# Where the weight pieces of a float32 decoder lie in SBUF: stationary hi and lo pieces moved to other places modulo 512 bytes

## The chip, the core and the metric

The kernel runs on one core of a Trainium2 chip. The metric is the device time of one execution in microseconds (us). Before the change it is 609.66 us, the median of three runs (609.53 to 610.31).

## What is computed

Two decoder layers over 256 tokens of width 1024, in float32, and a last RMSNorm. Each layer normalises its input and projects it by one wide matrix (1024 x 9808). Three attention mixers of 8 heads work on the result, their outputs are multiplied by SiLU gates, projected by a matrix per branch, weighted by sigmoid gates, summed, projected once more and added to the input. Cut to what matters here:

```python
def hybrid_layer(x, gain, w_in, f_bias, w_branch, w_out):
    h = rms_norm(x, gain)
    proj = jnp.einsum('bsd,de->bse', h, w_in)                 # 1024 x 9808
    (qa, ka, va, ga, qb, kb_, vb_, gb, qc, kc, vc, gc,
     q_idx, k_idx, w_idx, f_logit, merge_logit) = jnp.split(proj, SPLIT_POINTS, axis=-1)
    ...
    y = jnp.einsum('nbsw,nwd->bsnd', jnp.stack([oa, ob, oc], axis=0), w_branch)
    gates = jax.nn.sigmoid(merge_logit).reshape(B, S, N_BRANCH, D_MODEL)
    merged = jnp.sum(gates * y, axis=2)
    return x + jnp.einsum('bsd,de->bse', merged, w_out)
```

## The kernel before

**Hi and lo pieces.** Every float32 weight is split into two float32r pieces: ACT copies the raw weights to a hi piece (L415), DVE subtracts hi from raw and writes the rest as a lo piece (L419). Activations are split likewise (hTh and hTl for the normalised input, og0h, og0l, og1h, og1l for the branch outputs). A product then takes three matmuls: hi with hi, hi with lo, lo with hi.

**Buffers.** The hi pieces go through a ring of six tiles wh0 to wh5, the lo pieces through wl0 to wl5, each of 1152 float32r numbers per partition (4608 bytes), of which a piece takes 1024. The raw weights arrive by DMA from SyncE in four tiles of 2048 numbers. In the program as built, the wh tiles begin at byte 128 modulo 512 of a partition and the wl tiles at 0. The tiles hTh, hTl and og0h to og1l begin at 192 modulo 512, the tiles v0 and v1 at 128. Below, "at 128" always means the byte address modulo 512 at which an operand begins. One block of 128 columns is 512 bytes, so all blocks of a piece begin at the same place.

**Two ways to use a piece.** Where the tokens are the output's rows (units of unit_a, first_v and va_units: the v projections and the output projection), the activation is stationary and the weight piece streams past it as the moving operand. Their places in the tile are set by the table MOVING, read by shifted (L393). Where the tokens are the output's columns, the weight piece is stationary, in blocks of 128 x 128, and 256 columns of an activation stream. These are the B units (unit_b at L469: queries, keys, gates, index queries and merge gates, 64 units a layer, 24 matmuls each, pieces from win_b) and the Y units (unit_y at L956: branch projections, 24 a layer, 12 matmuls each, pieces from wbr). Their pieces have no entry in the table: piece (L398) puts them at the beginning of the tile, so the stationary hi blocks begin at 128 and the lo blocks at 0, and what streams begins at 192.

In both layers together 3,072 matmuls are of B units and 576 of Y units, 3,648 in all, 1,824 in each layer. Two thirds of them have a hi block as their stationary operand. Before each, TensorE loads that block (LDWEIGHTS), beside the streaming of the matmul before.

**What sets the order.** A planner in the kernel places every operation by its own costs, due times and a table of shifts. In a B unit the 16 hi matmuls and 8 lo matmuls are mixed by UNIT_ORDER:

```python
UNIT_ORDER = ((6, 1), (3, 1), (3, 2), (2, 1), (1, 2), (1, 1))
```

that is six matmuls with hi, one with lo, three with hi, one with lo, and so on. Between units, TensorE computes the scores (tiles s, L678 and L680), the transposes of the probabilities (tile t, L766) and the products with v (tile o, L782 to L785).

Of the kernel before, what the change touches and what calls it, by code (L numbers as in the profile page):

```python
# [32 lines left out]

R_RING = 6
R_RAW = 4
MOVING = {"V": (192, 192), "C": (128, 0), "CK": (384, 384), "O": (128, 128)}
TAIL = {"ACT": 95.0, "DVE": 85.0, "POOL": 0.0, "PE": 0.0, "SP": 0.0}
STEP = 24.0
SPLIT_LEAD = 2.0
# [237 lines left out]
def hybrid_trunk(ctx, tc, x, w_in, w_branch, w_out, final_gain, consts, out):  # L277
    nc = tc.nc
    PE, ACT, DVE, POOL = nc.tensor, nc.scalar, nc.vector, nc.gpsimd
# [13 lines left out]
    def T(b):  # L293
        return b.slot[1]
# [28 lines left out]
    V = [pool.tile([128, 2, 8, 128], F32R, name=f"v{i}") for i in range(2)]  # L323
# [67 lines left out]

    chunks, pieces = {}, {}

    def shifted(kind):
        at = MOVING[kind]
        return [slice((a - base) % 512 // 4, (a - base) % 512 // 4 + 1024) for a, base in zip(at, (128, 0))]

    def piece(key, ckey, ap, cshape, sel, shape, k, at=(slice(0, 1024), slice(0, 1024))):  # L398
        if key in pieces:
            return pieces[key]  # L400
        if ckey not in chunks:
            c = chunks[ckey] = Buf("raw")
            ca, cb = cshape

            def load():
                c.v = T(c)[:, :ca * cb].rearrange("p (a b) -> p a b", a=ca)
                nc.sync.dma_start(c.v, ap)
            dma(load, 512 * ca * cb * (1 if cb >= 128 else 2), [], [c], k - 12, f"dma {ckey}")
        c = chunks[ckey]
        a, b = shape  # L410
        p = pieces[key] = (Buf("wh"), Buf("wl"))

        def hi():
            p[0].v = T(p[0])[:, at[0]][:, :a * b].rearrange("p (a b) -> p a b", a=a)
            ACT.activation(p[0].v, sel(c.v), AF.Copy)  # L415

        def lo():
            p[1].v = T(p[1])[:, at[1]][:, :a * b].rearrange("p (a b) -> p a b", a=a)
            DVE.tensor_tensor(p[1].v, sel(c.v), p[0].v.bitcast(F32), op=ALU.subtract)  # L419
        act(hi, a * b, False, [c], [p[0]], k - SPLIT_LEAD, f"hi {key}")  # L420
        dve(lo, a * b, [c, p[0]], [p[1]], k - SPLIT_LEAD, f"lo {key}", port=True)
        return p
# [6 lines left out]
    def rows_a(kind, w, l, c0, i, k):  # L429
        src = w[l][(i // 2) * 512:(i // 2 + 1) * 512, c0:c0 + 512].rearrange("(k p) c -> p k c", p=128)  # L430
        a = (i % 2) * 2
        return piece((kind, l, c0, i), (kind, l, c0, i // 2), src, [4, 512], lambda r: r[:, a:a + 2, :], [2, 512], k,
                     shifted("O" if kind == "O" else "V"))

    def wbr(l, n, j, k):
        src = w_branch[l][n][:, (j // 2) * 256:(j // 2 + 1) * 256].rearrange("(k p) c -> p k c", p=128)
# [26 lines left out]
    def unit(name):  # L463
        units[0] += 1
        return units[0] - 1
# [560 lines left out]
    hA = (lambda k, t: hTh[:, k, t * 128:(t + 1) * 128], lambda k, t: hTl[:, k, t * 128:(t + 1) * 128])  # L1026
# [16 lines left out]

    def first_v():

        us, at = [unit("va0"), unit("va1")], shifted("V")
        ps = [Buf("proj"), Buf("proj")]
        left, done = [24, 24], [[], []]
        raws = [Buf("raw"), Buf("raw")]
        for i in range(KC):  # L1050
            c = raws[i // 4]
            if i % 2 == 0:
                ph, pl = Buf("wh"), Buf("wl")
            v = lambda b, w, i=i: T(b)[:, at[w]][:, (i % 2) * 512:(i % 2 + 1) * 512]
            rv = lambda c=c, i=i: T(c)[:, (i % 4) * 512:(i % 4 + 1) * 512]
            src = w_in[0][i * 128:(i + 1) * 128, COL["va"]:COL["va"] + 512]
            kr, kh, kl = Tok(), Tok(), Tok()
            plan.op([("SP", 512 * 512 / 330.0, lambda rv=rv, src=src: nc.sync.dma_start(rv(), src))], [], [kr], -95 + 0.2 * i, LAND,
                    f"dma va{i}", touch=[c])
            key = W_KEY[0] + W_KEY[1] * i  # L1060
            if i:
                key = max(key, HT_KEY[0] + HT_KEY[1] * (i - 0.5))
            plan.op([("ACT", t_act(512, False), lambda v=v, rv=rv, ph=ph: ACT.activation(v(ph, 0), rv(), AF.Copy)),
                     ("DVE", t_dve2(512), lambda v=v, rv=rv, ph=ph: DVE.tensor_copy(v(ph, 0), rv()))],
                    [kr], [kh], key, 0.0, f"hi va{i}", touch=[c, ph])
            dve(lambda v=v, rv=rv, ph=ph, pl=pl: DVE.tensor_tensor(v(pl, 1), rv(), v(ph, 0).bitcast(F32), op=ALU.subtract),
                512, [kr, kh], [kl], key + 0.05, f"lo va{i}", touch=[c, ph, pl], port=True)
            for t in range(2):
                for w, h, kw, kx, n in ((ph, hA[0], kh, 0, 0), (ph, hA[1], kh, 1, 0), (pl, hA[0], kl, 0, 1)):
                    def emit(t=t, w=w, h=h, i=i, v=v, n=n):  # L1070
                        left[t] -= 1
                        PE.matmul(T(ps[t]), h(i, t), v(w, n), start=left[t] == 23, stop=left[t] == 0)  # L1072
                    k = Tok()
                    done[t].append(k)
                    pe(emit, t_mm(512), [kw, k_hT[kx][t][i]], [k], us[t] - 10, f"va{t}", touch=[ps[t], w])
        for t in range(2):
            v_out(ps[t], t, 0, done[t], us[t])

    def va_units(l, vi):

        fine = False
        us, ats = [unit(f"vc{h}{t}") for h in "lr" for t in range(2)], [shifted("C"), shifted("CK")]

        def rows(raw, c, n, k0, k1, key):
            tok = Tok()
# [4 lines left out]
            return tok  # L1090

        def split(p, n, w, c, x0, x1, raw, cols, k0, reads, toks, key):
            dst = lambda i: T(p[i])[:, ats[w > 256][i]][:, :n * w].rearrange("p (k c) -> p k c", k=n)[:, x0:x1, c:c + cols]
            src = lambda: T(raw)[:, :8 * cols].rearrange("p (k c) -> p k c", k=8)[:, k0 + x0:k0 + x1]
            m = (x1 - x0) * cols
            ways = [("ACT", t_act(m, False), lambda: ACT.activation(dst(0), src(), AF.Copy))]
            if fine:
                ways.append(("DVE", t_dve2(m), lambda: DVE.tensor_copy(dst(0), src())))
            plan.op(ways, reads + [k_hT[1][0][KC - 1]], toks[0], key, 0.0, "hi va", touch=[raw, p[0]])
            dve(lambda: DVE.tensor_tensor(dst(1), src(), dst(0).bitcast(F32), op=ALU.subtract), m, reads + toks[0], toks[1],  # L1100
                key + 0.5, "lo va", touch=[raw, *p], port=True)

        for side, (w, slots) in enumerate(((256, ((0, 4), (4, 8))), (336, ((0, 3), (3, 6), (6, 8))))):
            u = us[2 * side:2 * side + 2]
            ps = [Buf("proj"), Buf("proj")]
            left, done = [24, 24], [[], []]
# [9 lines left out]
            for i, (a, b) in enumerate(slots):  # L1116
                p, n = [Buf("wh"), Buf("wl")], b - a
                tk = [[Tok() for _ in range(n)] for _ in range(2)]
                hk = VA_HI[2 * side + i] if fine else u[0] - SPLIT_LEAD
                for x0, x1 in ((0, 2), (2, 4)) if fine and not side and not i else ((0, n),):  # L1120
                    split(p, n, w, 0, x0, x1, raw, 256, a, list({id(kr[a + x]): kr[a + x] for x in range(x0, x1)}.values()),
                          [tk[0][x0:x1], tk[1][x0:x1]], hk)
                kt2 = [[Tok()], [Tok()]]
                if side:
                    split(p, n, w, 256, 0, n, rk, 80, a, [kk], kt2, hk)
                for t in range(2):
                    for wi, hi in ((0, 0), (0, 1), (1, 0)):
                        for js in [(x,) for x in range(n)] if fine and not side and not i else (range(n),):
                            def emit(t=t, wi=wi, hi=hi, js=js, p=p, n=n, a=a, w=w, ps=ps, left=left):
                                for x in js:  # L1130
                                    left[t] -= 1
                                    PE.matmul(T(ps[t])[:, :w], hA[hi](a + x, t), T(p[wi])[:, ats[w > 256][wi]][:, :n * w].rearrange(  # L1132
                                        "p (k c) -> p k c", k=n)[:, x], start=left[t] == 23, stop=left[t] == 0)
                            k = Tok()
                            done[t].append(k)
                            pe(emit, len(js) * (t_mm(w) + 4.6), [tk[wi][x] for x in js] + (kt2[wi] if side else []) +
                               [k_hT[hi][t][a + x] for x in js], [k], u[t] - (10 if fine else 0), f"v{side}{t}", touch=[ps[t], p[wi]])
# [44 lines left out]
    for l in range(L):  # L1182
# [31 lines left out]
        for hh in range(2):  # L1214
            gets = [lambda k, i=i: rows_a("O", w_out, l, hh * 512, i, k) for i in range(4)]
            for t in range(2):
                ra = [lambda k, p=p: [k_mg[k][p]] for p in range(2)]
                cols = [(0, 256), (256, 256)] if last and hh + t == 2 else [(0, 512)]
                for i, (c, n) in enumerate(cols):
                    u, ps = unit_a(f"o{hh}{t}", gets, t, mA[0], mA[1], ra, c, n)  # L1220
# [38 lines left out]
```

## Time and profile before

| | |
|---|---|
| median of 3 runs | 609.66 us (609.53 to 610.31) |
| time of the profiled execution | 609.88 us |
| its span, first to last instruction | 607.9 us |
| granted TensorE clock | 0.998 |
| matmuls, weight loads in the trace | 4848 each |
| HBM read | 103.42 MB |

The profiled execution is 0.22 us above the median. Its time is the span and 2.0 us around it. PE stands for TensorE's matmuls, PEld for its weight loads, which run beside them. Matmuls are pipelined: one that streams 256 columns is recorded as 276 ns long, but the next one starts 113 ns after it, so what a matmul costs is read from the distance between starts. Starts are given to a hundredth of a microsecond, and so a distance is read over several matmuls.

### The profile page before, as it was taken

The numbers are of one execution on the slowest core, as the hardware profiler recorded it, in microseconds if no ns is written. First come the engines' busy times: TensorE is split into PE (matmuls) and PEld (weight loads), VectorE is DVE, ScalarE is ACT, GpSimd is POOL, SyncE is SP. The second block draws the span as 40 slices with busy tenths as digits, with TensorE's granted clock in tenths as the row PEclk, the third lists the DMA queues.
The fourth block names the chain that finished last, engine by engine and source line by source line (L and its number), as shares of the span: only waits on it lengthen the run. The fifth ranks groups of instructions, "written<-read, shape, count | busy, mean of one in ns | idle before, by whom it ended". The sixth has DMA issues, their size and how long they took to land.

```text
span 607.9 us, 12752 instructions
## 1 busy us (share of the span) xinstructions
PE 599.9 (99%) x4848; PEld 581.7 (96%) x4848; DVE 534.3 (88%) x1340; ACT 439.9 (72%) x933; POOL 89.7 (15%) x97
## 2 busy tenths in 40 slices
PE   8999999999999999999999999999999999999996
PEld 6999999999998999999889999999999999999985
DVE  8899999997998899979586999999889978999873
ACT  6668669697986678775585875987788756986641
POOL 1032052000000334100000520320000014220000
PEclk9999999999999999999999999999999999999999
DMA  9995384845454655284547547557448256445411
GB/s 305 296 312 183 90 240 140 252 134 188 140 174 139 208 173 173 88 274 163 160 141 255 159 139 234 166 183 228 128 118 278 92 175 204 144 139 183 165 35 70
DMA packets 98109, 107.39 MB, mean 177 GB/s; under 512 B 4352, under 2 KB 88960, under 8 KB 98048
## 3 DMA queue, kind: packets, MB, share of 16 engines
q1 hardware_dynamic: 97760, 106.15, 55.4%
q8 instruction: 38, 0.62, 0.4%
q10 hardware_dynamic: 288, 0.43, 0.2%
q14 instruction: 23, 0.19, 0.1%
HBM read 103.42 MB, written 1.05 MB: 172 GB/s over the span
## 4 chain that ended last, share of the span: by engine, by line
PE 97%; issue 1%; DMA 1%; DVE 0%; ACT 0%; POOL 0%; POOLq 0%; DVEq 0%; SPq 0%
PE proj L457 80%; PE proj L1132 4%; PE t L766 3%; PE s L680 2%; PE s L678 2%; PE proj L1072 2%; PE o L785 1%; PE o L782 1%; DMA xg<-in_x_dram 1%; PE o L784 0%; PE o L783 0%; PE t L580 0%; PE s L580 0%; POOL fsum L626 0%; ACT tmp L565 0%
## 5 line engine op out<-in xcount | busy, mean ns | idle before, releaser
L457 PE MATMUL proj<-hTh,wh 128*128 128x256 f32 x1024 | 266.6, 278 | 0.0
L457 PE MATMUL proj<-hTl,wh 128*128 128x256 f32 x1024 | 265.8, 277 | 0.0
L419 DVE TENSOR_TENSOR wl<-raw,wh 128x1024 fp32r<-128x1024 f32 x180 | 221.9, 1240 | 29.1 <-ACT wh L415 26.5
L457 PE MATMUL proj<-hTh,wl 128*128 128x256 f32 x1024 | 230.6, 278 | 0.0
L415 ACT ACTIVATE wh<-raw 128x1024 fp32r<-128x1024 f32 x180 | 190.0, 1058 | 54.9 <-PE proj L457 50.2
L457 PEld LDWEIGHTS proj<-hTh,wh 128*128 128x128 f32 x1024 | 192.4, 188 | 0.1
L457 PEld LDWEIGHTS proj<-hTl,wh 128*128 128x128 f32 x1024 | 192.3, 188 | 0.1
L457 PEld LDWEIGHTS proj<-hTh,wl 128*128 128x128 f32 x1024 | 173.5, 188 | 0.0
L507 POOL TENSOR_TENSOR rsh<-rsh,cst 128x256 f32<-128x256 f32 x40 | 32.9, 823 | 323.4 <-DVE rsh L506 271.5
L509 POOL TENSOR_TENSOR rr<-rr,rsh 128x256 f32<-128x256 f32 x40 | 48.0, 1199 | 5.1 <-DVE rr L508 2.0
L743 ACT ACTIVATE e<-e,st 128x128 f32<-128x128 f32 (+1 forms) x96 | 42.7, 447 | 6.6 <-DVE st L739 6.3
L457 PE MATMUL proj<-wh,v 128*128 128x512 f32 (+1 forms) x144 | 35.2, 366 | 0.0
L457 PE MATMUL proj<-og0l,wh 128*128 128x256 f32 x128 | 33.8, 276 | 0.0
L457 PE MATMUL proj<-og0h,wh 128*128 128x256 f32 x128 | 32.3, 276 | 0.0
L457 PEld LDWEIGHTS proj<-wh,v 128*128 128x128 f32 x144 | 25.3, 189 | 4.2
L457 PE MATMUL proj<-og0h,wl 128*128 128x256 f32 x128 | 28.6, 276 | 0.0
L771 DVE TENSOR_TENSOR ptl<-t,pth 128x384 fp32r<-128x384 f32 x48 | 24.8, 550 | 0.7 <-ACT pth L769 0.5
L457 PEld LDWEIGHTS proj<-og0h,wh 128*128 128x128 f32 x128 | 24.0, 188 | 0.0
L457 PEld LDWEIGHTS proj<-og0l,wh 128*128 128x128 f32 x128 | 24.0, 188 | 0.0
L800 DVE TENSOR_TENSOR ot<-o,ot 64x256 f32<-64x256 f32 x48 | 19.9, 415 | 3.8 <-ACT ot L798 3.4
L769 ACT ACTIVATE pth<-t 128x384 fp32r<-128x384 f32 x48 | 21.8, 482 | 0.4
L457 PEld LDWEIGHTS proj<-og0h,wl 128*128 128x128 f32 x128 | 21.7, 188 | 0.0
(225 smaller groups left out, 1098.5 us busy)
## 6 DMA issues: line engine op xcount, KB each, us to landing
raw<-in_w_in_dram SPq DMA_DIRECT2D x74, 1024.0 KB, 5.3
raw<-in_w_branch_dram SPq DMA_DIRECT2D x24, 512.0 KB, 3.6
raw<-in_w_out_dram SPq DMA_DIRECT2D x8, 1024.0 KB, 5.1
raw<-in_w_in_dram SPq DMA_DIRECT2D x8, 256.0 KB, 5.4
tmp<-wf SPq DMA_DIRECT2D x16, 128.0 KB, 6.5
raw<-in_w_in_dram SPq DMA_DIRECT2D x2, 320.0 KB, 7.6
x<-in_x_dram SPq DMA_DIRECT2D x2, 256.0 KB, 4.9
acc<-in_final_gain_dram SPq DMA_DIRECT2D x1, 512.0 KB, 3.6
```

Source lines behind the costliest of these rows:

```text
L415: ACT.activation(p[0].v, sel(c.v), AF.Copy)
L419: DVE.tensor_tensor(p[1].v, sel(c.v), p[0].v.bitcast(F32), op=ALU.subtract)
L457: PE.matmul(o(), a(), b(), start=first and i == 0, stop=last and i == n - 1)
L507: gps(lambda: POOL.tensor_tensor(T(sh)[:np_], T(sh)[:np_], s[:np_], op=ALU.mult), S, [k_rope], [sh], key, "rope")
L509: gps(lambda: POOL.tensor_tensor(T(r)[:np_], T(r)[:np_], T(sh)[:np_], op=ALU.add), S, [sh], [r], key, "rope")
L678: PE.matmul(o.rearrange("p (h c) -> p h c", h=2), qh[:, sl], kl[:, :, :n], start=True, stop=False)
L743: act(lambda t=t, a=a, n=n, e=e, st=st: ACT.activation(T(e)[:, a:a + n], T(e)[:, a:a + n], AF.Exp, bias=T(st)[:, t:t + 1], scale=-1.0, acc ...
L766: PE.transpose(T(ps)[:, i * 128:(i + 1) * 128], T(es[h])[:, i * 128:(i + 1) * 128], ident)
L769: act(lambda h=h, src=src: ACT.activation(T(ph)[:, h], src(), AF.Copy), 384, True, [ps], [kp[h][0]], key, "pT", touch=[ph])
L771: dve(lambda h=h, src=src: DVE.tensor_tensor(T(pl)[:, h], src(), T(ph)[:, h].bitcast(F32), op=ALU.subtract), 384, [ps, kp[h][0]], [kp[h][1 ...
L800: dve(lambda r=r, h=h: DVE.tensor_tensor(T(t)[r], T(o)[:64, h * S:(h + 1) * S], T(t)[r], op=ALU.add), S, [o], [kt[h]], key, "og", touch=[t ...
L1132: PE.matmul(T(ps[t])[:, :w], hA[hi](a + x, t), T(p[wi])[:, ats[w > 256][wi]][:, :n * w].rearrange("p (k c) -> p k c", k=n)[:, x], start=le ...
```

## The change

The table MOVING becomes PLACE, with an entry for each layer, and gets two more kinds: "B" and "Y", the stationary pieces. Their hi pieces now begin at 0 modulo 512 in both layers, their lo pieces at 128 in the first layer and at 64 in the second. The entries of the moving pieces (V, C, CK, O0, O1) repeat the old numbers in both layers. The function place gives the part of the tile from the wanted place to its end, and piece looks the place up by the kind of its key.

```diff
-MOVING = {"V": (192, 192), "C": (128, 0), "CK": (384, 384), "O": (128, 128)}
+PLACE = {"V": ((192, 192), (192, 192)),
+         "C": ((128, 0), (128, 0)),
+         "CK": ((384, 384), (384, 384)),
+         "O0": ((128, 128), (128, 128)),
+         "O1": ((128, 128), (128, 128)),
+         "B": ((0, 128), (0, 64)),
+         "Y": ((0, 128), (0, 64))}
...
-    def shifted(kind):
-        at = MOVING[kind]
-        return [slice((a - base) % 512 // 4, (a - base) % 512 // 4 + 1024) for a, base in zip(at, (128, 0))]
-
-    def piece(key, ckey, ap, cshape, sel, shape, k, at=(slice(0, 1024), slice(0, 1024))):
+    def place(kind, l):
+        at = PLACE[kind][l]
+        return [slice((a - base) % 512 // 4, 1152) for a, base in zip(at, (128, 0))]
+
+    def piece(key, ckey, ap, cshape, sel, shape, k):
+        at = place(key[0] if key[0] in PLACE else "V", key[1])
...
-        return piece((kind, l, c0, i), (kind, l, c0, i // 2), src, [4, 512], lambda r: r[:, a:a + 2, :], [2, 512], k,
-                     shifted("O" if kind == "O" else "V"))
+        return piece((f"{kind}{c0 // 512}" if kind == "O" else kind, l, c0, i), (kind, l, c0, i // 2), src, [4, 512], lambda r: r[:, a:a + 2, :], [2, 512], k)
```

The rest of the diff carries the layer to place in first_v and va_units. As built, the two programs are the same instruction for instruction on every engine, waits included: only addresses inside the wh and wl tiles differ. Stationary operands, before and after:

| stationary block | place before | place after, layer 1 | place after, layer 2 | matmuls per layer |
|---|---|---|---|---|
| hi, B and Y units | 128 | 0 | 0 | 1,216 |
| lo, B and Y units | 0 | 128 | 64 | 608 |

What streams past them begins at 192 before and after.

More of the change, by code (lines that the diff above doesn't have):

```diff
@@ L1044, in first_v @@
     def first_v():
-        us, at = [unit("va0"), unit("va1")], shifted("V")
+        us, at = [unit("va0"), unit("va1")], place("V", 0)
         ps = [Buf("proj"), Buf("proj")]
@@ L1081, in va_units, with rows_of @@
         fine = False
-        us, ats = [unit(f"vc{h}{t}") for h in "lr" for t in range(2)], [shifted("C"), shifted("CK")]
+        us = [unit(f"vc{h}{t}") for h in "lr" for t in range(2)]
+        def rows_of(p, i, n, w):
+            at = place("C" if w == 256 else "CK", l)[i]
+            return T(p[i])[:, at][:, :n * w].rearrange("p (k c) -> p k c", k=n)
         def rows(raw, c, n, k0, k1, key):
@@ L1092, in split @@
         def split(p, n, w, c, x0, x1, raw, cols, k0, reads, toks, key):
-            dst = lambda i: T(p[i])[:, ats[w > 256][i]][:, :n * w].rearrange("p (k c) -> p k c", k=n)[:, x0:x1, c:c + cols]
+            dst = lambda i: rows_of(p, i, n, w)[:, x0:x1, c:c + cols]
             src = lambda: T(raw)[:, :8 * cols].rearrange("p (k c) -> p k c", k=8)[:, k0 + x0:k0 + x1]
@@ L1131, in emit @@
                                     left[t] -= 1
-                                    PE.matmul(T(ps[t])[:, :w], hA[hi](a + x, t), T(p[wi])[:, ats[w > 256][wi]][:, :n * w].rearrange(
-                                        "p (k c) -> p k c", k=n)[:, x], start=left[t] == 23, stop=left[t] == 0)
+                                    PE.matmul(T(ps[t])[:, :w], hA[hi](a + x, t), rows_of(p, wi, n, w)[:, x], start=left[t] == 23, stop=left[t] == 0)
                             k = Tok()
```

## The prediction

> **What bounds the kernel now.** I read the page first, for the engine that sets the end.
>
> ```profile
> span 607.9 us, 12752 instructions
> PE 599.9 (99%) x4848; PEld 581.7 (96%) x4848; DVE 534.3 (88%) x1340; ACT 439.9 (72%) x933; POOL 89.7 (15%) x97
> PE 97%; issue 1%; DMA 1%; DVE 0%; ACT 0%; POOL 0%; POOLq 0%; DVEq 0%; SPq 0%
> ```
>
> PE is 97% of the chain that ended last, so time is gained or lost only where a matmul starts earlier or later. Next, the groups of PE by line, since the change touches one kind of matmul alone: those with wh or wl behind the comma, as the stationary operand.
>
> ```profile
> L457 PE MATMUL proj<-hTh,wh 128*128 128x256 f32 x1024 | 266.6, 278 | 0.0
> L457 PE MATMUL proj<-hTl,wh 128*128 128x256 f32 x1024 | 265.8, 277 | 0.0
> L457 PE MATMUL proj<-hTh,wl 128*128 128x256 f32 x1024 | 230.6, 278 | 0.0
> L457 PE MATMUL proj<-og0l,wh 128*128 128x256 f32 x128 | 33.8, 276 | 0.0
> ```
>
> These are the 3,072 matmuls of the B units and, with og, some of the 576 of the Y units. The last number before the bar's end is the mean duration of one. It is 276 to 278 ns for the same shape, so something makes some of them longer. The third view, all instructions on a tile in one stretch (minimum, median, maximum), tells when. First a stretch without scores or transposes:
>
> ```profile
> L457 PE MATMUL proj<-hTh,wh x51: 276/276/276, 200.0 to 219.9; 128*128 128x256 f32 x51
> L457 PE MATMUL proj<-hTl,wh x50: 276/276/276, 200.1 to 219.7; 128*128 128x256 f32 x50
> ```
>
> Then the microsecond behind a group of scores:
>
> ```profile
> L457 PE MATMUL proj<-hTh,wh x5: 278/279/280, 56.9 to 57.9; 128*128 128x256 f32 x5
> L457 PE MATMUL proj<-hTl,wh x4: 277/279/279, 57.0 to 57.8; 128*128 128x256 f32 x4
> ```
>
> The same instructions with the same places take 276 ns in the one and 279 in the other. The timeline of both shows what that does to the starts. The quiet stretch (first column: start):
>
> ```profile
> 200.00 0.28 PE L457 MATMUL proj<-hTh,wh 128*128 128x256 f32 x1
> ...
> 202.04 0.28 PE L457 MATMUL proj<-hTh,wl 128*128 128x256 f32 x1
> ```
>
> Here 18 matmuls start in 2.04 us: 113.3 ns each. And behind the scores:
>
> ```profile
> 56.86 0.28 PE L457 MATMUL proj<-hTh,wh 128*128 128x256 f32 x1
> 56.98 0.28 PE L457 MATMUL proj<-hTl,wh 128*128 128x256 f32 x1
> ...
> 57.45 0.28 PE L457 MATMUL proj<-hTl,wh 128*128 128x256 f32 x1
> 57.57 0.28 PE L457 MATMUL proj<-hTh,wl 128*128 128x256 f32 x1
> ...
> 57.92 0.28 PE L457 MATMUL proj<-hTh,wh 128*128 128x256 f32 x1
> 58.04 0.28 PE L457 MATMUL proj<-hTh,wl 128*128 128x256 f32 x1
> 58.15 0.28 PE L457 MATMUL proj<-hTl,wh 128*128 128x256 f32 x1
> 58.26 0.28 PE L457 MATMUL proj<-hTh,wh 128*128 128x256 f32 x1
> 58.38 0.28 PE L457 MATMUL proj<-hTl,wh 128*128 128x256 f32 x1
> ```
>
> From 56.86 to 58.04 ten matmuls start in 1.18 us: 118 ns each, 4.7 more than in the quiet stretch. From 58.04 on they start 113.3 ns apart again (three in 0.34 us). So there are two ways of running, a quiet one at 113.3 ns and bursts at 118. A burst begins where TensorE comes back from scores, transposes or products with v, and this one ends at the second matmul whose stationary operand is a lo block (58.04), not at the first (57.57). A lo block is the only thing in a burst that lies at another place, 0 instead of 128.
>
> Do places matter at all? Two stretches in which weights stream and the activation is stationary, also 256 columns, never become quiet:
>
> ```profile
> 21.24 0.63 PE L1132 MATMUL proj<-wh,hTh 128*128 128x256 f32 x4
> ...
> 24.07 0.63 PE L1132 MATMUL proj<-wh,hTh 128*128 128x256 f32 x4
> ```
>
> ```profile
> 596.31 0.64 PE L457 MATMUL proj<-wh,v 128*128 128x256 f32 x4
> ...
> 598.46 0.64 PE L457 MATMUL proj<-wh,v 128*128 128x256 f32 x4
> ```
>
> In the first, 24 matmuls take 2.83 us, 117.9 ns each, with the moving operand at 128 or 0 and the stationary one at 192. In the second, 18 take 2.15 us, 119.4 each, with both at 128. With the moving operand at 192 and the stationary one at 128 or 0, as in B and Y units, it stays quiet for 20 us. Distances from the stationary to the moving place of 64 and 192 bytes allow 113.3 ns; of 0, 448 and 320 (modulo 512) they were only seen at 118 to 120.
>
> **The change, part by part.** It adds and removes no instruction. Three parts have a price.
>
> *The quiet stretches.* After the change the distance is 192 for hi blocks and 64 for lo blocks in layer 1. Both were seen quiet, so I take 113.3 ns, nothing gained or lost. In layer 2 the lo blocks have a distance of 128, which no row shows with 256 columns. Its neighbours on both sides, 64 and 192, are quiet, so I take 0. The other end is 4.7 ns on each of the 608 lo loads of layer 2, 2.9 us, or on all its 1,824 matmuls, 8.6 us. A gain is excluded: no row shows a shorter distance than 113.3.
>
> *The bursts.* All that can be won is what the bursts cost now. The hTl row gives it, since its mean of 277 lies 1 ns above the quiet 276. Its rows over most of the span have no exceptionally long matmul, while those of hTh do:
>
> ```profile
> L457 PE MATMUL proj<-hTh,wh x1008: 276/276/365, 39.9 to 568.5; 128*128 128x256 f32 x168
> L457 PE MATMUL proj<-hTl,wh x1008: 276/276/285, 40.1 to 568.9; 128*128 128x256 f32 x168
> ```
>
> So 3,072 x 1 ns = 3.1 us, and as the mean is rounded, 1.5 to 4.6. Adding up the distances between starts of these 3,648 matmuls beyond 113.3 ns, record by record without the 42 long ones (362 to 365 ns, behind transposes, which no place explains), gives 2.2 us of excess. I use 2.2, as it is in the unit that counts. In a burst a hi block loaded behind a hi block keeps the 4.7 ns every time; the change of place that comes with a lo block is what ends it. After the change these steps exist in the same positions, with the opposite sign in layer 1 (0 to 128 and back instead of 128 to 0 and back) and half as large in layer 2. Bounds: if a load at 0 does not keep the distance of 118 ns, hardly a burst outlives its second matmul, and nearly all 2.2 us go; if the steps no longer end it, a burst lasts until its unit group ends, which is the end of 8.6 us a layer. Between them I take a quarter off the bursts, 0.55 us: two loads in three now lie where the burst above ended, which speaks for shorter bursts, and against it, that burst outlived its first load at 0.
>
> *The splits.* ACT and DVE write the pieces at the new places.
>
> ```profile
> L419 DVE TENSOR_TENSOR wl<-raw,wh 128x1024 fp32r<-128x1024 f32 x180 | 221.9, 1240 | 29.1 <-ACT wh L415 26.5
> L415 ACT ACTIVATE wh<-raw 128x1024 fp32r<-128x1024 f32 x180 | 190.0, 1058 | 54.9 <-PE proj L457 50.2
> ```
>
> ACT idles 50.2 us ahead of the hi pieces because PE has not yet given a tile back: the ring of six is full, and that is the cover. DVE's 29.1 us are a wait for ACT. Even 50 ns more on each of 180 pieces would be 9 us, less than that cover. I take 0. If the cover were gone, those 9 us would come into PE's path.
>
> The sum against the profiled execution: 609.88 - 0.55 = 609.3; against the median of the runs, which is 0.22 lower, 609.1 us.
>
> **A rule that speaks against any effect.** The rows above show 113.3 ns against 118 and 119.4 for the same number of columns. The Trainium skill, SBUF — State Buffer, "Who interferes with whom", lists two independent read ports for PE, one for the moving operand and one for LDWEIGHTS, and says that PE never waits on anyone. By that rule the places are free and the sum is 609.7 instead of 609.1; the trace agrees in the quiet stretch and does not explain the bursts. As a mechanism of this kernel it is the first rival.
>
> **The rivals.**
>
> *Places do nothing.* The bursts would then be the tail of every switch of operation: the pipeline needs some matmuls to get its lead back, whatever lies where. For it: a burst begins at a switch, and at the same places TensorE runs at 118 and then at 113.3. Against it: two stretches with other places never become quiet. Time 609.7. Chance 0.15.
>
> *The bursts go.* A load at 0 ends a burst at once, now that every hi block lies there. For it: the burst above ends with a load at 0. Against it: its first load at 0 did not end it. It gives 1.3 to 2.2 us, 607.5 to 608.4, most likely 607.9. Chance 0.32.
>
> *The 118 ns settle, in layer 2 above all.* The step between hi and lo is only 64 bytes there, and a burst that a step of 128 bytes needed two tries to end may then run through; or the untested distance of 128 is one of those that never become quiet. For it: the two stretches that stay at 118 or 119 have steps of 128 and of 0 between their pieces, so a step alone is no way out. Against it: both neighbours of the distance are quiet. Price 4.7 ns a matmul: 2.9 us if a third of layer 2 runs so, 612.5 us; 8.6 if all of it is. It decides from 260 matmuls on (1.2 us / 4.7 ns), 7% of the 3,648. Chance 0.20.
>
> That the change doesn't reach the hardware is excluded: the built program has the stationary blocks at the new places.
>
> **How the numbers follow.** A measurement of this kernel can tell about 0.2%, 1.2 us, from no change. My forecast, that bursts change by less than half and the rest stays, has 0.33, and lies inside 0.2% as does the first rival: same 0.48. The likeliest time is the forecast's, 609.1 us, its own range 608.4 to 610.4. Faster by over 0.2% is the second rival alone, 0.32; slower the third, 0.20. The range reaches down to 607.6, near the end of the second rival, since no more than the bursts can be won, and leaves some 0.05 below. Above it reaches 611.5, which takes in bursts that are almost doubled (1.8 us) and leaves the larger part of the third rival out, some 0.13.
>
> **What would show it.** Right: in the changed kernel's profile the stretch from 200 to 220 us has 276/276/276 again, the mean of the hTl row lies between 276 and 277, and PE's span is a few tenths of a microsecond shorter. For the second rival: the ten matmuls behind the scores near 56.9 us start 113 ns apart from the second one on. For the third: layer 2 (from some 310 us) has medians of 279 on wh or wl where layer 1 has 276. The splits would be wrong if PE waited for ACT or DVE at L457. The prediction is wrong if the median leaves 607.6 to 611.5, and its reasoning is wrong if the time falls by more than 2.2 us, since nothing here shows more to win.

## The result, and the profile after

The changed kernel takes 616.61 us (median of four runs, 616.4 to 616.73), the kernel before beside it 609.75: a ratio of 1.011 (95% interval 1.009 to 1.013). It is 6.9 us slower. The forecast was 609.1 us in a range of 607.6 to 611.5, so it was wrong, in its sign too.

The page of the changed kernel, the same rows as before:

```profile
span 614.5 us, 12752 instructions
PE 607.5 (99%) x4848; PEld 589.2 (96%) x4848; DVE 535.8 (87%) x1340; ACT 440.0 (72%) x933; POOL 89.4 (15%) x97
PE 97%; issue 1%; DMA 1%; DVE 0%; POOL 0%; ACT 0%; POOLq 0%; DVEq 0%; SPq 0%
```

PE is busy 7.6 us longer with the same 4848 matmuls and is still 97% of the chain; the span grew by 6.6 us. One microsecond of the 7.6 costs nothing: the 24 matmuls on the tile ones, with which PE begins, are recorded as 5.49 us instead of 4.51, and what follows them starts at 6.70 us in both. DVE and ACT are busy within 1.5 us of what they were, and PE waits for them no more than it did. All that PE waited for, by line (us in total, times, longest), before:

```profile
PE t L580 <- ACT tmp L565: 1.1, 1, 1.1
PE t L993 <- DVE ones L988: 1.1, 1, 1.1
```

After:

```profile
PE t L999 <- DVE ones L994: 1.1, 1, 1.1
PE t L586 <- ACT tmp L571: 0.2, 1, 0.2
```

So the loss lies in the matmuls themselves. The groups by line put the time on the stationary pieces: their means rise from 278, 277 and 278 ns to 280, 279 and 279.

```profile
L463 PE MATMUL proj<-hTh,wh 128*128 128x256 f32 x1024 | 268.9, 280 | 0.0
L463 PE MATMUL proj<-hTl,wh 128*128 128x256 f32 x1024 | 267.9, 279 | 0.0
L463 PE MATMUL proj<-hTh,wl 128*128 128x256 f32 x1024 | 232.8, 279 | 0.0
```

A mean over both layers hides where. The busy times by stretch tell it; after the stretch and its length come PE's busy time and, in brackets, how many matmuls fall into the stretch, then the granted clock, the DMA share and GB/s. The first stretch lies in layer 1, the second in layer 2. Before:

```profile
34.00:303.00 269.00, 269.00 (x2234) 1.00 0.57 178
331.00:580.00 249.00, 249.00 (x2146) 1.00 0.55 172
```

After:

```profile
34.00:303.00 269.00, 269.00 (x2234) 1.00 0.57 178
331.00:580.00 249.00, 249.00 (x2089) 1.00 0.54 170
```

In the 269 us of layer 1 PE does exactly as many matmuls as before. In the 249 us of layer 2 it does 57 fewer, and 57 x 113.3 ns are 6.5 us: nearly the whole loss. A stretch of layer 2 without scores or transposes shows what it looks like. Before (minimum, median, maximum of the duration):

```profile
L457 PE MATMUL proj<-hTl,wh x49: 276/276/279, 500.1 to 519.9; 128*128 128x256 f32 x49
```

After:

```profile
L463 PE MATMUL proj<-hTl,wh x49: 276/281/286, 500.0 to 519.8; 128*128 128x256 f32 x49
L463 PE MATMUL proj<-hTh,wl x49: 276/279/284, 499.9 to 519.7; 128*128 128x256 f32 x49
```

Matmuls with hi blocks (wh) and with lo blocks (wl) are both longer, by their medians of 281 and 279, though the hi pieces lie at 0 in both layers. In the timeline of the same stretch the starts come 117.5 ns apart (20 in 2.35 us) instead of 113.3:

```profile
500.12 0.28 PE L463 MATMUL proj<-hTh,wh 128*128 128x256 f32 x1
...
502.47 0.28 PE L463 MATMUL proj<-hTl,wh 128*128 128x256 f32 x1
```

In layer 1 the stretch from 200 to 220 us has its 276 ns again, as the prediction asked:

```profile
L463 PE MATMUL proj<-hTl,wh x50: 276/276/276, 200.1 to 219.7; 128*128 128x256 f32 x50
```

In what follows, "excess" of a layer is the sum over its B and Y matmuls of what the distance between two starts has beyond 113.3 ns, the long ones behind transposes left out, as in the prediction. Before the change it is 1.13 us in layer 1 and 1.09 in layer 2; after it, 1.07 and 7.61. The difference of 6.46 us is the span's 6.6 but for 0.1. What is left of the profiled time without both excesses is 607.7 us in both kernels.

### The profile page after: what moved, and what is told of

Its sections match the earlier page's. It is cut to its first block, busy times and chain, and to the rows that moved or that the text cites. A ratio compares the mean times of both kernels' runs of the same rounds, so it can differ in the third digit from the quotient of the medians.

```text
span 614.5 us, 12752 instructions
## 1 busy us (share of the span) xinstructions
PE 607.5 (99%) x4848; PEld 589.2 (96%) x4848; DVE 535.8 (87%) x1340; ACT 440.0 (72%) x933; POOL 89.4 (15%) x97
## 4 chain that ended last, share of the span: by engine, by line
PE 97%; issue 1%; DMA 1%; DVE 0%; POOL 0%; ACT 0%; POOLq 0%; DVEq 0%; SPq 0%
PE proj L463 80%; PE proj L1142 4%; PE t L772 3%; PE s L686 2%; PE s L684 2%; PE proj L1078 2%; PE o L791 1%; PE o L788 1%; DMA xg<-in_x_dram 1%; PE o L790 0%; PE o L789 0%; PE t L586 0%; PE s L586 0%; POOL fsum L632 0%; DVE tmp L530 0%
## 5 line engine op out<-in xcount | busy, mean ns | idle before, releaser
L463 PE MATMUL proj<-hTh,wh 128*128 128x256 f32 x1024 | 268.9, 280 | 0.0
L463 PE MATMUL proj<-hTl,wh 128*128 128x256 f32 x1024 | 267.9, 279 | 0.0
L463 PE MATMUL proj<-hTh,wl 128*128 128x256 f32 x1024 | 232.8, 279 | 0.0
L463 PEld LDWEIGHTS proj<-hTl,wh 128*128 128x128 f32 x1024 | 192.6, 188 | 0.1
L463 PEld LDWEIGHTS proj<-hTh,wh 128*128 128x128 f32 x1024 | 192.5, 188 | 0.1
L463 PEld LDWEIGHTS proj<-hTh,wl 128*128 128x128 f32 x1024 | 174.1, 188 | 0.0
L463 PE MATMUL proj<-wh,v 128*128 128x512 f32 (+1 forms) x144 | 35.2, 366 | 0.0
L463 PE MATMUL proj<-og0l,wh 128*128 128x256 f32 x128 | 34.1, 278 | 0.0
L463 PE MATMUL proj<-og0h,wh 128*128 128x256 f32 x128 | 32.5, 278 | 0.0
L463 PEld LDWEIGHTS proj<-wh,v 128*128 128x128 f32 x144 | 25.3, 189 | 4.3
L463 PE MATMUL proj<-og0h,wl 128*128 128x256 f32 x128 | 28.9, 278 | 0.0
L463 PEld LDWEIGHTS proj<-og0h,wh 128*128 128x128 f32 x128 | 24.1, 188 | 0.0
L463 PEld LDWEIGHTS proj<-og0l,wh 128*128 128x128 f32 x128 | 24.0, 188 | 0.0
L804 ACT ACTIVATE ot<-o 64x256 f32<-64x256 f32 x48 | 18.2, 380 | 5.4 <-PE o L791 4.6
```

The lines of the kernel that those rows point to most:

```text
L463: PE.matmul(o(), a(), b(), start=first and i == 0, stop=last and i == n - 1)
L804: act(lambda r=r, h=h: ACT.activation(T(t)[r], T(o)[64:, h * S:(h + 1) * S], AF.Copy), S, True, [o], [kt[h]], key, "og", touch=[t], half=True)
```

## The experiments

Each kernel is the changed one with other places. A distance is the moving place less the stationary one. "Distance theory": what costs is a stationary block 128 bytes from the moving place. Its rivals: the step of 64 bytes between hi and lo pieces; hi pieces at 0; the second layer itself; the place as such, wherever the moving operand lies.

The first and the last kernel ran ten times, the others once, so for those the excesses carry the argument more than the times. The two agree: the profiled time without both excesses is 607.3 to 608.0 us in every kernel but the one that moves what streams, where it is 608.5.

### Lo pieces at 128 in both layers

```diff
-         "B": ((0, 128), (0, 64)),
-         "Y": ((0, 128), (0, 64))}
+         "B": ((0, 128), (0, 128)),
+         "Y": ((0, 128), (0, 128))}
```

> Lo pieces at 128 in the second layer too; hi at 0 in both. Distance theory (a lo block 128 bytes below the moving place is what costs): the second layer falls back to the first one's excess of about 1.1 us, the time to 609.7 us, 6.5 us under the changed kernel. Step theory (hi and lo 64 bytes apart is what costs): the same, as the step is 128 again. Hi theory (hi at 0 is at fault, only hidden in the first layer): the second layer stays at 616 to 617 us.

Measured: 609.59 us, a ratio to the kernel before of 0.9997 (0.9988 to 1.0007), excess 1.14 and 0.95 us. The lo pieces at 64 in layer 2 are the whole loss. Hi at 0 is not at fault. Distance and step theory both forecast this and are not yet told apart. Hi at 0 with lo at 128 is as fast as hi at 128 with lo at 0.

### The layers swapped

```diff
-         "B": ((0, 128), (0, 64)),
+         "B": ((0, 64), (0, 128)),
```

and "Y" likewise, here and below.

> Lo pieces at 64 in the first layer, at 128 in the second; hi at 0. Distance and step theory alike: the excess of some 7.6 us moves to the first layer, the second has about 1.1 us, time about 616.5 us. Theory that something else in the second layer makes it sensitive: both layers about 1.1 us, time 609.7 us.

Measured: 615.92 us, excess 7.68 and 0.94 us. The loss moved with the entry. First layer, then second:

```profile
L463 PE MATMUL proj<-hTl,wh x512: 276/281/286, 33.9 to 278.0; 128*128 128x256 f32 x171
L463 PE MATMUL proj<-hTl,wh x512: 276/276/285, 337.2 to 574.9; 128*128 128x256 f32 x171
```

Nothing in the second layer itself is sensitive.

### Hi and lo at one place: 0 and 64, 128 and 192

```diff
+         "B": ((0, 0), (64, 64)),
```

> Hi and lo at the same place: both at 0 in the first layer (distance 192 to the moving operand), both at 64 in the second (distance 128). Distance theory: the first layer stays quiet (excess 0.5 to 1.5 us), the second has every load at distance 128 and is at least as slow as in the changed kernel (7.6 to 8.6 us): time 616 to 618 us. Step theory: no step of 64 bytes is left, so the second layer is as quiet as the first, about 609.7 us. Theory that steps are what end a burst: both layers stay at 118 ns from their first burst on, some 8 us each, time 622 to 625 us.

```diff
+         "B": ((128, 128), (192, 192)),
```

> Hi and lo at the same place: both at 128 in the first layer (distance 64), both at 192 in the second (distance 0). Distance theory: first layer quiet (0.5 to 1.5 us of excess), second at 119.4 ns throughout as the output projection with both operands at 128, that is 1,824 x 6.1 ns = 11.1 us: time 619 to 621 us. Step theory: both layers quiet, 609 to 610 us. Theory that steps end a burst: both slow, 8 to 11 us each, time 624 to 628 us.

Measured: 620.54 us with excesses of 2.90 (place 0) and 10.00 us (place 64); 626.8 us with 7.44 (place 128) and 11.80 us (place 192). The rows of the first kernel, layer 1 and layer 2:

```profile
L463 PE MATMUL proj<-hTl,wh x512: 275/277/284, 34.2 to 273.9; 128*128 128x256 f32 x171
L463 PE MATMUL proj<-hTl,wh x512: 274/282/291, 332.6 to 579.0; 128*128 128x256 f32 x171
```

and of the second:

```profile
L463 PE MATMUL proj<-hTl,wh x512: 276/279/283, 34.3 to 278.1; 128*128 128x256 f32 x171
L463 PE MATMUL proj<-hTl,wh x500: 278/283/286, 337.3 to 579.9; 128*128 128x256 f32 x167
```

The step theory falls: with no step between hi and lo, a distance of 128 is worse than in the changed kernel (10.0 us for 7.6). The distance theory missed too: it gave the first layers 0.5 to 1.5 us, and they have 2.9 (distance 192) and 7.4 (distance 64). In the kernel before two thirds of the blocks lie at a distance of 64 and the rest at 192, with 1.1 us in a layer, so each of the two alone is worse than both together.

The starts show how. Take as a stretch the B and Y matmuls between two other operations of TensorE, 44 in layer 1. At 192 alone the burst at its beginning is over after at most four matmuls in 29 of them, and lasts to the end in the other 15, of 6 to 204 matmuls. At 64 alone no burst ends: three stretches, of 36, 78 and 24 matmuls, run at 113.3 ns from their beginning, and the others at 118 to their end. Two stretches of the kernel with 64 alone, the second of them a quiet one:

```profile
L463 PE MATMUL proj<-hTl,wh x61: 279/280/280, 202.3 to 226.1; 128*128 128x256 f32 x61
L463 PE MATMUL proj<-hTl,wh x16: 276/276/276, 239.8 to 244.9; 128*128 128x256 f32 x16
```

With both distances, in the kernel before and in the one with lo at 128 in both layers, no burst lasts beyond 12 matmuls. So two things are needed. The distances must be ones that allow 113.3 ns, as 64 and 192 do and 128 and 0 do not. And in these runs a burst of more than four matmuls ended only where the distance changes between them. The theory that steps end a burst gave 8 us or more to a layer without a step; it fails by that number at 192 and nearly holds at 64, and the second kernel's time lies in its 624 to 628 us.

### What streams is moved by 64 bytes

```diff
+    pool.tile([128, 16], F32, name="pad0")
     hTh = pool.tile([128, KC, S], F32R, name="hTh")
...
+    pool.tile([128, 112], F32, name="pad1")
     NBD = 3
...
+         "B": ((64, 192), (0, 128)),
```

> What streams is moved: hTh, hTl and the four og tiles begin at 256 instead of 192; all other tiles stay. First layer: hi at 64, lo at 192, distances 192 and 64 as in the fast first layer of the changed kernel. Second layer: hi at 0, lo at 128, distances 256 and 128. Distance theory: the first layer has 0.9 to 1.5 us of excess although its hi blocks lie at 64; the second is slow, 6 us or more, although its places are those that were fast. Place theory (a stationary block at 64 is slow wherever the moving operand lies): the first layer is slow (7 us or more), the second fast (about 1 us). The v projections, with hT now at 256, may move by some tenths of a microsecond. Time 615 to 617 us by either.

Measured: 619.94 us, excess 1.50 and 9.90 us. First layer, then second:

```profile
L465 PE MATMUL proj<-hTl,wh x512: 275/276/285, 34.2 to 272.9; 128*128 128x256 f32 x171
L465 PE MATMUL proj<-hTl,wh x512: 274/282/287, 331.9 to 578.4; 128*128 128x256 f32 x171
```

The place theory falls. Hi blocks at 64 are fast here, and the places 0 and 128, fast together in the runs above, are slow. What counts is the distance between the two operands of TensorE, the stationary block and the columns that stream. Whether it is the block in use or the one being loaded for the next matmul is not told apart. The time missed the 615 to 617 us expected by either theory: layer 2 has 9.9 us, as its other distance, 256, is bad as well, which the next runs show. And the v projections, whose activation moved too, are slower: 36 matmuls of 512 columns in layer 1 start 233.2 ns apart at their new distance of 192, and 226.8 ns at a distance of 0 in the changed kernel.

### The other half of the 512 bytes

```diff
+         "B": ((256, 256), (320, 320)),
```

> Hi and lo at one place: both at 256 in the first layer (distance 448), both at 320 in the second (distance 384). Distance theory with a period of 512 bytes: 448 was 117.9 ns where weights stream, so some 4.6 ns for every load, 8 us in each layer: time 623 to 625 us. A period of 256 bytes: 448 is the same as 192 and 384 the same as 128, so 2.9 us of excess in the first layer and 10.0 in the second: time about 620.5 us.

```diff
+         "B": ((384, 384), (448, 448)),
```

> Hi and lo at one place: both at 384 in the first layer (distance 320), both at 448 in the second (distance 256). Period of 512 bytes: 320 was 118 ns where weights stream, so 7 to 8.5 us of excess in the first layer; 256 lies between 192 (2.9 us) and 320, so 3 to 8 in the second: time 618 to 624 us. Period of 256 bytes: 320 is the same as 64 (7.4 us) and 256 the same as 0 (11.8 us): time about 626.8 us.

Measured: 620.84 us, excess 2.92 and 10.00 us; 626.74 us, excess 7.44 and 11.80 us. These are the numbers of places 0, 64, 128 and 192 again, to 0.02 us. The period is 256 bytes, not 512.

### Hi at distance 128, lo at a good one, and the reverse

```diff
+         "B": ((64, 0), (128, 64)),
```

> First layer: hi at 64, lo at 0 (distances 128 and 192). Second layer: hi at 128, lo at 64 (distances 64 and 128). Distance theory: both layers are slow; in the first two loads in three are at the bad distance, so 7 to 10 us of excess; in the second one in three, 6 to 8 us, as in the changed kernel. Theory that the lo block alone must not lie at distance 128, because it is what ends a burst: first layer 1 to 3 us, second 6 to 8 us.

Measured: 624.62 us, excess 9.24 and 7.88 us. Two blocks in three at a distance of 128 cost more than one in three. The theory that only the lo block matters falls, as the first layer has its lo blocks at a distance of 192. The second layer says less of 128, since its hi blocks lie at a distance of 64, which alone costs 7.4 us.

### Distances between the steps of 64

```diff
+         "B": ((32, 32), (480, 480)),
```

> Hi and lo at one place between the 64-byte steps: both at 32 in the first layer (distance 160), both at 480 in the second (distance 224 modulo 256). Theory that the distance modulo 256 sets a price that changes smoothly: 160 lies between 128 (10.0 us of excess) and 192 (2.9), 224 between 192 and 0 (11.8): 4 to 9 us each, time 616 to 625 us. Theory that only the 64-byte block counts: 160 is in the block of 128, so 10.0 us, and 224 in that of 192, so 2.9 us (or the other way round, as the moving place is itself on a 64-byte edge): time about 620.5 us.

```diff
+         "B": ((0, 192), (0, 32)),
```

> Hi at 0 (distance 192) in both layers; lo at 192 in the first (distance 0) and at 32 in the second (distance 160). If one bad lo distance is enough to keep a layer at 118 ns, as 128 does: first layer 7 to 11 us of excess, the second between 1 and 8, by how bad 160 is. If any step from 192 and back ends a burst and only 128 is special: 1 to 2 us in both, time 609.5 to 611 us.

```diff
+         "B": ((0, 480), (480, 0)),
```

> Distances 192 and 224 mixed: hi at 0 and lo at 480 in the first layer, the other way round in the second. If 224 alone is as bad as 0: 6 us or more of excess in the first layer, 8 or more in the second, 622 us or more. If it is as good as 192: 1 to 3 us each, 609.5 to 613.5 us, and if a small step ends bursts better than one of 128 bytes, under 0.9 us in a layer.

Measured: 625.55 us (excess 8.62 and 8.91), 624.7 us (8.51 and 8.57) and 624.16 us (7.99 and 8.77). Distances of 160 and 224 are bad, alone and with 192, and so is 0 with 192; the theory that only the 64-byte block counts falls, since 160 and 224 cost about the same, 4.8 and 4.9 ns a matmul. That a price between two steps lies between theirs (4 to 9 us) fits both layers of the first of the three, the time just missing its 625 us. In the second, the excess of layer 2 is above the 8 us expected. The tries, by distance modulo 256 (several rows are from the second layer of a kernel):

| distances of hi and lo | excess in a layer, us |
|---|---|
| 64 and 192 (before) | 1.1 |
| 192 and 64 (lo at 128) | 0.9 to 1.1 |
| 192 and 64, all moved by 64 bytes | 1.5 |
| 192 and 192 | 2.9 |
| 64 and 64 | 7.4 |
| 192 and 128 (the change, layer 2) | 7.6 |
| 64 and 128; 128 and 192 | 7.9; 9.2 |
| 192 and 0; 192 and 160; 192 and 224; 224 and 192 | 8.5; 8.6; 8.0; 8.8 |
| 160 and 160; 224 and 224 | 8.6; 8.9 |
| 0 and 128 (all moved by 64 bytes) | 9.9 |
| 128 and 128 | 10.0 |
| 0 and 0 | 11.8 |

Only 64 and 192 together let the 113.3 ns hold but for short bursts, whichever is hi; 192 alone does so for 29 of 44 stretches, and 64 alone for three.

### The rule on the side of the streaming weights

```diff
-         "O1": ((128, 128), (128, 128)),
+         "O1": ((128, 128), (320, 192)),
+         "B": ((0, 128), (0, 128)),
```

> Stationary pieces as in the run with lo at 128 in both layers. In the second layer's output projection, second half, the streaming weights move from 128 and 128 to 320 (hi) and 192 (lo), so that they begin 192 and 64 bytes past the stationary operand at 128 instead of 0. There 47 matmuls of 256 columns near the end started 119.4 to 120 ns apart. If the distance rule holds for the moving side too: they come to 113.3 ns after a burst of some matmuls, 0.1 to 0.3 us less, time 609.3 to 609.6 us. If a burst that begins with the first of them does not end, as at the v projections with 128 and 0 past 192: 118 ns, under 0.1 us less, 609.6 us. A difference of 0.3 us is not measurable in the time; the distances between starts decide.

Measured: 609.65 us, ratio 0.9997 (0.9987 to 1.0007). Timeline near the end, distances of 192 and 64 between streaming weights and stationary operand:

```profile
590.57 1.09 PE L463 MATMUL proj<-wh,v 128*128 128x512 f32 x4
...
594.73 1.08 PE L463 MATMUL proj<-wh,v 128*128 128x512 f32 x4
...
596.11 0.63 PE L463 MATMUL proj<-wh,v 128*128 128x256 f32 x4
...
598.93 0.63 PE L463 MATMUL proj<-wh,v 128*128 128x256 f32 x4
```

and the same part of the kernel before, with a distance of 0:

```profile
590.87 1.07 PE L457 MATMUL proj<-wh,v 128*128 128x512 f32 x4
...
594.95 1.07 PE L457 MATMUL proj<-wh,v 128*128 128x512 f32 x4
```

The 24 matmuls from 596.11 to 598.93 start 117.5 ns apart; with a distance of 0 it was 119.4. They are a little better and never become quiet, which is the second of the two expectations. And the 18 of 512 columns ahead of them went from 226.7 ns (4.08 us) to 231.1 ns (4.16 us): for them a distance of 0 is the better one, as in the run that moved what streams. What the one shape wins the other loses. So on this side the pair of 192 and 64 does not bring 113.3 ns about.

No place tried beats both kernels: the best, lo at 128 in both layers, measures the same as the kernel before.

## Why the prediction was wrong

*What bounds the kernel.* Right: PE is the chain before and after, no wait took part, and the loss lies wholly in the distance between the starts of matmuls with stationary pieces.

*The quiet stretches.* This is the step that failed: "In layer 2 the lo blocks have a distance of 128, which no row shows with 256 columns. Its neighbours on both sides, 64 and 192, are quiet, so I take 0." The price of a distance need not lie between those of its neighbours. With all blocks at one distance, 128 costs 10.0 us, 64 and 192 cost 7.4 and 2.9. 128 is bad whether a third of the blocks lies there (7.6 us), two thirds (9.2) or all (10.0), and so are 160 and 224, which lie nearer to 192. Nor were the neighbours good by themselves: each allows 113.3 ns, but at 64 alone no burst ends, and at 192 alone a third of them do not. The trace of before held only the pair, and I read it as two good values.

The other end of that bound was right. It was 2.9 us if only the 608 lo loads paid and 8.6 if all 1,824 matmuls did; measured 6.5 us more than before. It came nearer to the second, because the hi blocks, though at 192, do not become quiet among lo blocks at 128: in the changed kernel's layer 2 the distance between starts is on average 4.2 ns too long, 5.5 where a lo block follows hi, and 4.4 where hi follows hi, which is what a burst at 192 alone costs.

*The reading of the stretches at 118 and 119 ns.* Wrong in part. "Distances ... of 0, 448 and 320 (modulo 512) they were only seen at 118 to 120" was taken to mean that those distances are bad. The period is 256, so 448 and 320 are the pair of 192 and 64, which is the good one where weights are stationary. The stretch of 48 matmuls of 256 columns at 21.2 us ran at 118 ns from beginning to end all the same, and the last run's at 192 and 64 stayed at 117.5; why is open. At 0 no stretch of 256 columns was quiet.

*The bursts.* The size was right, 2.2 us for both layers together, and no run won more. The quarter taken off did not come: in layer 1, where hi and lo have changed their distances, the excess went from 1.13 to 1.07 us. A burst of the changed kernel near 56.9 us, the place shown before:

```profile
56.84 0.28 PE L463 MATMUL proj<-hTh,wh 128*128 128x256 f32 x1
...
57.43 0.28 PE L463 MATMUL proj<-hTl,wh 128*128 128x256 f32 x1
...
58.33 0.28 PE L463 MATMUL proj<-hTl,wh 128*128 128x256 f32 x1
```

Five matmuls at 118 ns, and from 57.43 on eight in 0.90 us, 112.5 with the rounding of the view: shorter than before here, longer elsewhere. "The change of place that comes with a lo block is what ends it" holds in part: with one place a burst of more than four matmuls never ended, but at a distance of 192 two thirds ended earlier without any change.

*The splits.* Right: PE waits for neither ACT nor DVE at L463.

*The rivals.* The third was what happened, by its second half: the untested distance never becomes quiet (in layer 2 at most five starts in a row keep to 113 ns). Its price was worked out as 8.6 us if all of layer 2 is slow; the runs give 6.5. The range should have reached up to it, since both ends of an unseen row were on the page and the likelier one had been chosen by a neighbour alone. The first rival, that places do nothing, falls with the first two experiments: same instructions in the same order, and 6 us come and go with one number. According to the distance between its stationary and its streaming operand a matmul of 256 columns costs 0.5 to 6.5 ns beyond 113.3; the loads themselves stay at a median of 188 ns in the stretch from 500 to 520 us, before and after. The Trainium skill, SBUF — State Buffer, "Who interferes with whom", lists PE's two read ports as independent; the measurements here, where the places of the two operands decide 6 us and more, differ from that, and they decide.

*What stays open.* Why 64 and 192 allow two ways of running, 113.3 and 118 ns, and why a change between them ends a burst. Distances alone do not decide it: at the same distances the streaming weights of the v projections stay at 118 and the B units do not. The cause on the chip was not measured, only that the cost follows the distance between the two operands with a period of 256 bytes, shown for four distances and with what streams at two places. Distances that are no multiple of 32 were not tried, nor what they do beside other tile sizes.

## What to carry to other kernels

Where TensorE loads a block of 128 x 128 float32r beside every 256 streaming columns, the start addresses of the two operands relative to each other are worth a sweep: here the kernel ranged from 609.6 to 626.8 us with the same instructions. Sweep them in pairs and all over, by putting another value in each layer, as a value that lies between two good ones can be bad, and two values can be good only together. And where a prediction rests on a row that the profile does not have, both ends belong in the range, not the neighbour's value.

## What the runs showed of the hardware

With a weight load of 128 x 128 beside every 256 streaming columns, the distance between the starts of matmuls depends on the distance of the two operands' start addresses modulo 256 bytes. With all blocks at one distance the mean excess over 113.3 ns was 1.6 ns at 192, 4.1 at 64, 4.8 at 160, 4.9 at 224, 5.5 at 128 and 6.5 at 0; with 64 and 192 mixed, 0.5 to 0.6.

At the same addresses there are two ways of running, 113.3 and 118 ns. With 64 alone a burst at 118 ns never ended within its stretch, with 192 alone within four matmuls or not at all, and with both after at most 13 matmuls.

For 512 columns against one load, a distance of 0 was best (226.7 ns, against 231.1 at 192 and 64, and 233.2 at 192).
